# Splitting all weights but four lead-in blocks, and the attention output, in a planned two-layer trunk on one core

## The chip, the cores and the metric

The kernel runs on one core of a Trainium2 chip. The metric is the device time of one execution in microseconds (us), as the median of several runs. A core has five engines that work side by side, each through its own instructions in their written order: TensorE (PE, matrix products; its weight loads are listed as PEld), VectorE (DVE), ScalarE (ACT), GpSimd (POOL) and SyncE (SP, which here issues nearly all DMAs). They meet through semaphores.

## The reference

Two layers of a decoder trunk on 256 tokens of width 1024. Each layer mixes tokens by two attentions side by side (NSA and MoBA, 8 heads of 64 each), merges them by sigmoid gates, and then runs a SwiGLU block of inner width 2816:

```python
for l in range(DEPTH):                                        # 2
    ada = jax.nn.silu(c) @ w_ada[l] + b_ada[l]
    sh_m, sc_m, g_m, sh_f, sc_f, g_f = jnp.split(ada[:, None, :], 6, axis=-1)
    h = rms_norm(x, norm_mix[l]) * (1.0 + sc_m) + sh_m
    (...) = jnp.split(h @ w_in[l], split_at, axis=-1)         # 4888 columns
    y_a = nsa_mixer(...)                                      # 256 x 512
    y_b = moba_mixer(...)                                     # 256 x 512
    gate_a, gate_b = jnp.split(jax.nn.sigmoid(g_br), 2, axis=-1)
    merged = gate_a * (y_a @ w_up_nsa[l]) + gate_b * (y_b @ w_up_moba[l])
    x = x + g_m * (merged @ w_out[l])
    h = rms_norm(x, norm_ffn[l]) * (1.0 + sc_f) + sh_f
    gt, up = jnp.split(h @ w_ffn_in[l], 2, axis=-1)
    x = x + g_f * ((jax.nn.silu(gt) * up) @ w_ffn_out[l])
```

All of it is in 32-bit floats.

## The kernel before

**Units and the two kinds of product.** Tokens lie in two tiles of 128 (t = 0, 1). Weights come from memory in units of 1 MB (128 partitions x 2048), for example four k-blocks of 128 rows by 512 columns, and each k-block times one token tile is one product of 128 x 128 by 128 x 512, added up in a PSUM bank. `load_unit` brings a unit into a tile `raw`. There are two ways on from there:

- A *split* unit goes through `split_unit`: ACT writes `hi`, the weights rounded to the reduced float type fp32r (L631), and DVE writes `lo` = raw - hi (L583). The other operand is kept as such a pair too (`hp` for the normalised input, `mT` for the merged attention, `aT` for the SwiGLU output). `mm3` then makes three fp32r matmuls for one product: hi x hi, hi x lo and lo x hi (L662).
- A *whole* unit is used as it was loaded, in one full fp32 matmul (also L662, in the groups as `raw`), with an operand that is whole too: `hd` for the input, `yy` for the attention output.

Whole are: blocks 0, 2, 4 and 6 of the eight blocks of the lead-in (`WHOLE`), three units of layer 0's input projection (`WHOLE_UNITS`: the second k-half of the columns from 2328, 2840 and 3352), and all eight units of the up-projections (w_up_nsa and w_up_moba, two column halves, two layers). The attention output is copied from PSUM to `yy` by ACT or DVE, whichever the plan gives it to (`evac`, L640 and L641).

**Tiles.** The large tiles (8 KB per partition) are 17 places of an arena, shared by kinds: raw, hi and lo have three places each that any unit may use, and two spare ones for hi and lo (one for raw) that only loads marked `spare` may use, those of w_out and the first of w_ffn_in among them. `yy` takes the first free of places 11 to 14. `aw` holds pieces of w_ada, whose dot products with silu(c) (`ada_dot`, DVE L589) are spread over the program.

**Stages.** In the lead-in, x is normalised (DVE and ACT; the power -0.5 on POOL, L970), silu(c) is spread over all partitions as `crow`, and the eight blocks of w_in's first 1816 columns are multiplied while their share of w_ada is dotted. Then the compression MLP (reads `e`), the rest of w_in (queries, keys, values, gates), both attentions, the up-projections (stage `ups`), w_out, and the FFN; layer 1 goes the same way. While a softmax goes through DVE, ACT and POOL, PE works on weight units of other columns.

**What sets the order.** Operations are recorded first. A planner (`Program.order`) then simulates the engines with a duration for every operation, picks at each step by priority, chooses between the engines that an operation allows, fills PE's planned gaps with matmuls on zeros (`fill`, L456), replays its plan with drawn DMA delays, raises priorities where PE had to wait, and does so 60 times. The best plan is written out engine by engine. So every duration in the planner moves instructions everywhere.

Of the kernel before, what the change touches and what calls it, by code (L numbers as in the profile page):

```python
# [17 lines left out]
P = 128  # L18
# [100 lines left out]
class Op:  # L119
    def __init__(self, no, alts, key):  # L120
        self.no, self.alts, self.key = no, alts, key
        self.preds, self.succs, self.acc, self.new = {}, [], [], []
        self.bytes = 0
        self.level = 0.0
        self.stage, self.first, self.boost = None, False, 0.0
        self.func, self.loads, self.parts, self.paced, self.then = None, None, False, False, None
# [5 lines left out]
FIRST = 1000.0  # L132
LAT = {"PE": 0.24, "DVE": 0.09, "ACT": 0.09, "POOL": 0.2, "SP": 0.0, "Q": 0.0}
# [5 lines left out]
class Program:  # L139
# [9 lines left out]
    SWITCH = (0.0, 0.0, 0.1)  # L149
# [116 lines left out]
    def order(self):  # L266
# [24 lines left out]
        parts = False  # L291
# [43 lines left out]
        while left:  # L335
# [6 lines left out]
            for op in ready:  # L342
# [15 lines left out]
            for e, cs in per.items():  # L358
# [44 lines left out]
            if e == "PE":  # L403
                parts = op.parts
# [14 lines left out]
            else:  # L419
                free[e] = t + c  # L420
# [21 lines left out]

    def fill(self, t0, t1):
# [15 lines left out]
        op.stage = "fill"  # L459
# [20 lines left out]
    def replay(self, steps, seed):  # L480
# [4 lines left out]
        dma, table, parts, gaps = 0.0, (), False, []  # L485
        for i, (e, op, c, deps) in enumerate(steps):
# [5 lines left out]
            if e == "PE":  # L492
                if op.stage != "fill" and op.parts != parts:
                    parts = op.parts
                    idle += self.SWITCH[2]
# [13 lines left out]
            free[e] = t + c  # L509
# [49 lines left out]
class Engines:  # L559
# [25 lines left out]
    def stt(self, out, a, s, b, op0, op1, accum=None):  # L585
# [5 lines left out]
                  [a, s, b], [out] + list(kw.values()), extra=0.08 if kw else 0.0)  # L591

    def ttr(self, out, a, b, op0, op1, init, accum):
        self._vec(("DVE",), cols(out), True,
                  lambda v: v.tensor_tensor_reduce(AP(out), AP(a), AP(b), 1.0, init, op0, op1, AP(accum)),  # L595
                  [a, b], [out, accum], extra=0.08)

    def ts(self, out, a, s1, s2, op0, op1=None, engs=("DVE",)):
# [3 lines left out]
                  [a, s1, s2], [out], psum=self._psum(a))  # L602
# [12 lines left out]
    def act(self, out, a, func, scale=None, bias=None, accum=None, late=()):  # L615
# [27 lines left out]
    def mm(self, out, lhsT, rhs, start, stop, cost=None):  # L643
# [6 lines left out]
        op.parts = AP(lhsT).shape[0] < P or AP(out).shape[0] < P  # L650

    def term(self, out, lhsT, rhs, first):
# [13 lines left out]
        self.p.op({"PE": (cost, [go])}, [lhsT, rhs], [out], term=s)  # L666

    def tr(self, out, a, ident):
        self.p.op({"PE": (0.109, [lambda: self.nc.tensor.transpose(AP(out), AP(a), AP(ident))])}, [a, ident], [out])  # L669

    def dma(self, out, src, q="SP", least=60000):
# [5 lines left out]
        eng = {"SP": self.nc.sync, "POOL": self.nc.gpsimd}[q]  # L677
        return self.p.op({q: (0.43 if q == "SP" else 0.6, [lambda: eng.dma_start(AP(out), AP(src))])},  # L678
# [5 lines left out]
WHOLE_UNITS = {(0, c, 1) for c in (2328, 2840, 3352)}  # L684


HALVED = 1
# [15 lines left out]
def trunk_kernel(tc, pools, A):  # L703
# [33 lines left out]
    NB = 17  # L737
# [16 lines left out]
    arena("yy", (11, 12, 13, 14), inturn=True)  # L754
# [373 lines left out]
    def lead_in(bs, h, W):  # L1128
# [16 lines left out]
        dma(vecs, A["vecs"], q="POOL")  # L1145
# [68 lines left out]
    def sublayer_mix(l, h):  # L1214
# [4 lines left out]
        ev, kv_, qv, vv, yv = (R.val(x_) for x_ in ("e", "kk", "qq", "ve", "yy"))  # L1219
# [185 lines left out]
        def softmax_T(s, t, nh, rq_small, cols_, gate):  # L1405
# [21 lines left out]
            alts["ACT"] = (nh * (0.295 + nk / 1200),  # L1427
# [47 lines left out]
        def nsa(t):  # L1475
# [43 lines left out]
            yaT[t] = whole_piece(quarter(yv, t, t), y)  # L1519

        def moba(t):
# [31 lines left out]
            ybT[t] = whole_piece(quarter(yv, 2 + t, 2 + t), y)  # L1553
# [72 lines left out]
        log_soon([yv, *tgv.values()])  # L1626
# [8 lines left out]
    def resid(l, t, c, b, g, e0=0, e1=512):  # L1635
# [3 lines left out]
        with R.ahead():  # L1639
            tt(r, b.of(e0)[:, e0:e1] if e1 - e0 < 512 else b, g[:, cs_], ALU.mult)  # L1640
# [6 lines left out]
    def sublayer_ffn(l, h):  # L1647
# [153 lines left out]
```

## Time and profile before

| | |
|---|---|
| median of 3 runs | 816.95 us (816.85 to 820.06) |
| span of the profiled execution | 815.4 us |
| granted TensorE clock | 1.000 |
| PE, busy share of the span | 99% |
| weight loads (PEld) | 75% |
| DVE | 71% |
| ACT | 50% |
| POOL | 10% |
| DMA moved | 183.82 MB, 225 GB/s on average |

The profiled execution's own time is known as its span, from the first to the last instruction; the median of the runs is 1.55 us above it. In the rows of the trace, a group names line, engine, operation and tiles (out<-in, without their numbers), then how many, their busy time, the mean of one, and the engine's idle time before them with what ended it. A timeline row gives start and length in us. Matmuls are pipelined: their lengths overlap, so the time of one is read from the distance between starts. A full fp32 matmul has two records.

### The profile page before, as it was taken

The numbers are of one execution on the slowest core, as the hardware profiler recorded it, in microseconds if no ns is written. First come the engines' busy times: TensorE is split into PE (matmuls) and PEld (weight loads), VectorE is DVE, ScalarE is ACT, GpSimd is POOL, SyncE is SP. The second block draws the span as 40 slices with busy tenths as digits, with TensorE's granted clock in tenths as the row PEclk, the third lists the DMA queues.
The fourth block names the chain that finished last, engine by engine and source line by source line (L and its number), as shares of the span: only waits on it lengthen the run. The fifth ranks groups of instructions, "written<-read, shape, count | busy, mean of one in ns | idle before, by whom it ended". The sixth has DMA issues, their size and how long they took to land.

```text
span 815.4 us, 10543 instructions
## 1 busy us (share of the span) xinstructions
PE 803.8 (99%) x3997; PEld 610.0 (75%) x3997; DVE 580.2 (71%) x1025; ACT 410.3 (50%) x654; POOL 79.5 (10%) x75
## 2 busy tenths in 40 slices
PE   8999999999999999999999999999999999999997
PEld 4567656764878888888878887676477888889886
DVE  6889977677986877777788898776377526545454
ACT  5445366662673534433585566587347524433441
POOL 4702620000100000000000442000000000000000
PEclk9999999999999999999999999999999999999999
DMA  9967585538949887977855785540391645555441
GB/s 357 416 230 290 161 295 182 175 130 310 372 152 338 311 305 288 327 293 259 311 174 214 278 289 180 188 151 25 104 344 69 210 153 174 202 192 207 151 158 52
DMA packets 74018, 183.82 MB, mean 225 GB/s; under 512 B 4304, under 2 KB 9696, under 8 KB 73456
## 3 DMA queue, kind: packets, MB, share of 16 engines
q1 hardware_dynamic: 73920, 183.08, 63.0%
q8 instruction: 31, 0.51, 0.2%
q14 instruction: 19, 0.16, 0.1%
q0 software_dynamic: 48, 0.08, 0.0%
HBM read 182.10 MB, written 1.05 MB: 225 GB/s over the span
## 4 chain that ended last, share of the span: by engine, by line
PE 88%; DVE 4%; DMA 2%; ACT 2%; POOL 2%; issue 1%; SPq 0%; DVEq 0%; POOLq 0%
PE bank L662 77%; PE bank L648 6%; PE bank L669 5%; DMA rows<-in_rows 1%; DVE tmp L583 1%; DMA raw<-in_w_out 1%; DVE lo L583 1%; POOL tmp L601 1%; DVE tmp L601 1%; ACT hp L631 1%; ACT hi L631 1%; SPq L678 0%; POOL tmp L583 0%; POOL at L1431 0%; DVE e L583 0%
## 5 line engine op out<-in xcount | busy, mean ns | idle before, releaser
L662 PE MATMUL bank<-hi,hp 128*128 128x512 f32 (+2 forms) x1296 | 359.2, 384 | 2.2 <-DVE hp L583 1.5
L583 DVE TENSOR_TENSOR lo<-raw,hi 128x2048 fp32r<-128x2048 f32 (+2 forms) x107 | 240.4, 2261 | 104.7 <-ACT hi L631 103.8
L631 ACT ACTIVATE hi<-raw 128x2048 fp32r<-128x2048 f32 (+2 forms) x107 | 200.6, 1891 | 223.1 <-PE bank L662 181.9
L662 PEld LDWEIGHTS bank<-hi,hp 128*128 128x128 f32 x1296 | 234.1, 188 | 59.1 <-issue 7.0
L662 PE MATMUL bank<-lo,hp 128*128 128x512 f32 (+2 forms) x648 | 208.2, 383 | 0.3 <-DVE lo L583 0.2
L662 PEld LDWEIGHTS bank<-lo,hp 128*128 128x128 f32 x648 | 119.3, 188 | 24.1 <-issue 2.6
L589 DVE SCALAR_TENSOR_TENSOR aw<-aw,crow 128x1024 f32<-128x1024 f32 x80 | 96.2, 1220 | 7.5 <-DMA aw<-in_w_ada 7.3
L662 PE MATMUL bank<-hi,aT 128*128 128x512 f32 (+1 forms) x364 | 100.7, 387 | 0.0
L662 PEld LDWEIGHTS bank<-hi,aT 128*128 128x128 f32 x364 | 66.6, 188 | 13.5 <-ACT hi L631 1.0
L662 PE MATMUL bank<-raw,yy 128*128 128x512 f32 x128 | 58.7, 596 | 0.7 <-ACT yy L640 0.7
L662 PE MATMUL bank<-lo,aT 128*128 128x512 f32 (+1 forms) x182 | 58.0, 385 | 0.0
L662 PE MATMUL bank<-raw,hd 128*128 128x512 f32 (+1 forms) x112 | 49.6, 568 | 0.9 <-ACT hd L631 0.9
L662 PEld LDWEIGHTS bank<-raw,yy 128*128 128x128 f32 x128 | 23.0, 190 | 23.7 <-issue 21.8
L662 PE MATMUL bank<-hi,mT 128*128 128x512 f32 x128 | 39.9, 403 | 0.1
L662 PEld LDWEIGHTS bank<-lo,aT 128*128 128x128 f32 x182 | 34.1, 188 | 6.1
L669 PE MATMUL bank<-ident,tmp 128*128 128x128 f32 x256 | 37.5, 274 | 1.2 <-DVE tmp L985 0.7
L631 ACT ACTIVATE at<-at,nb,rqa 128x128 f32<-128x128 f32 (+1 forms) x64 | 34.2, 536 | 7.5 <-DVE nb L589 7.5
L669 PEld LDWEIGHTS bank<-ident,tmp 128*128 128x128 f32 x256 | 30.4, 140 | 9.8 <-issue 1.8
L595 DVE CUSTOM_DVE_ANT_0 at<-bank,maskf 128x128 f32<-128x128 f32 (+1 forms) x96 | 29.5, 352 | 11.3 <-PE bank L669 8.9
L662 PEld LDWEIGHTS bank<-raw,hd 128*128 128x128 f32 x112 | 20.6, 189 | 17.2 <-issue 13.4
L583 DVE TENSOR_TENSOR tmp<-tmp,bank 128x512 f32<-128x512 f32 (+1 forms) x24 | 15.1, 639 | 22.0 <-PE bank L662 21.5
L631 ACT ACTIVATE tmp<-bank 128x512 f32<-128x512 f32 (+2 forms) x43 | 20.7, 509 | 16.3 <-PE bank L662 7.0
(185 smaller groups left out, 731.3 us busy)
## 6 DMA issues: line engine op xcount, KB each, us to landing
raw<-in_w_ffn_in SPq DMA_DIRECT2D x44, 1024.0 KB, 6.3
aw<-in_w_ada SPq DMA_DIRECT2D x80, 512.0 KB, 5.7
raw<-in_w_in SPq DMA_DIRECT2D x30, 1024.0 KB, 5.2
raw<-in_w_ffn_out SPq DMA_DIRECT2D x22, 1024.0 KB, 4.9
raw<-in_w_out SPq DMA_DIRECT2D x8, 1024.0 KB, 6.2
raw<-in_w_in SPq DMA_DIRECT2D x8, 908.0 KB, 9.1
sa<-in_w_ada SPq DMA_DIRECT2D x7, 1024.0 KB, 11.9
raw<-in_w_up_nsa SPq DMA_DIRECT2D x4, 1024.0 KB, 6.2
```

Of the source, the lines that this page charges most:

```text
L583: self._vec(engs, cols(out), True, lambda v: v.tensor_tensor(AP(out), AP(a), AP(b), op=op), [a, b], [out])
L589: lambda v: v.scalar_tensor_tensor(AP(out), AP(a), AP(s), AP(b), op0=op0, op1=op1, **{k: AP(x) for k, x in kw.items()}),
L595: lambda v: v.tensor_tensor_reduce(AP(out), AP(a), AP(b), 1.0, init, op0, op1, AP(accum)),
L601: lambda v: v.tensor_scalar(AP(out), AP(a), AP(s1), AP(s2), op0=op0, **kw),
L631: op = self.p.op({"ACT": (c, [lambda: self.nc.scalar.activation(AP(out), AP(a), func, **{k: AP(x) for k, x in kw.items()})])}, reads + lis ...
L648: op = self.p.op({"PE": (cost, [lambda: self.nc.tensor.matmul(AP(out), AP(lhsT), AP(rhs), start=start, stop=stop)])}, [lhsT, rhs], [out])
L662: self.nc.tensor.matmul(AP(out), AP(lhsT), AP(rhs), start=first, stop=v.gone == v.terms)
L669: self.p.op({"PE": (0.109, [lambda: self.nc.tensor.transpose(AP(out), AP(a), AP(ident))])}, [a, ident], [out])
```

## The change

It does six things. `WHOLE_UNITS` becomes empty and the up-projections' units are loaded split (`UPS_WHOLE`). The attention output is written as a pair by `split_into` (ACT writes hi, DVE lo), in two tiles `yy`, for which the arena gets an 18th place. The constants `vecs` are loaded through ACT's queue instead of POOL's. The planner gets other durations: a cost for each change of the matmul's shape in partitions, 0.08 and 0.1 us by which DVE and ACT take the next operation before the last one's result is there, and other costs of single operations. The last quarter of the result, which was multiplied in two halves of 256 columns, is multiplied in one piece of 512 again, and only its final scaling and adding stay halved. And the memory set aside for descriptors of software DMAs is cut to 2048 bytes.

```diff
+OVER = {"PE": 0.0, "DVE": 0.08, "ACT": 0.1, "POOL": 0.0, "SP": 0.0, "Q": 0.0}
...
-    SWITCH = (0.0, 0.0, 0.1)
+    TURN, SLACK, TALL = 0.15, 0.0, 0.05
+    FLAT, STICK = (P, P), 0.0
...
+            if e == "PE" and op.forms:
+                if op.forms[0] != form:
+                    t = max(t, free[e] + self.turn(form, op.forms[0]))
+                form = op.forms[1]
...
-                free[e] = t + c
+                free[e] = t + c - OVER[e]
...
-        eng = {"SP": self.nc.sync, "POOL": self.nc.gpsimd}[q]
-        return self.p.op({q: (0.43 if q == "SP" else 0.6, [lambda: eng.dma_start(AP(out), AP(src))])},
+        eng = {"SP": self.nc.sync, "ACT": self.nc.scalar}[q]
+        return self.p.op({q: (0.43 if q == "SP" else 0.15, [lambda: eng.dma_start(AP(out), AP(src))])},
...
-WHOLE_UNITS = {(0, c, 1) for c in (2328, 2840, 3352)}
+WHOLE_UNITS = set()
+UPS_WHOLE = (False, False)
...
-    NB = 17
+    NB = 18
...
-    arena("yy", (11, 12, 13, 14), inturn=True)
+    arena("yy", (17, 11, 12, 13, 14), inturn=True)
...
-        dma(vecs, A["vecs"], q="POOL")
+        dma(vecs, A["vecs"], q="ACT")
...
-        def whole_piece(d, src):
-            evac(d, src)
-            return [(None, None, d[:, j * P:(j + 1) * P]) for j in range(4)]
+        yl = None if UPS_WHOLE[l] else R.val("yy", dt=F32R)
+
+        def y_pieces(i, src):
+            d = quarter(yv, i, i)
+            if yl is None:
+                evac(d, src)
+                return [(None, None, d[:, j * P:(j + 1) * P]) for j in range(4)]
+            return split_into(d, quarter(yl, i, i), src)
...
-            yaT[t] = whole_piece(quarter(yv, t, t), y)
+            yaT[t] = y_pieces(t, y)
...
-                u = load_unit(A[w][l][:, cs_], 4, 512, True)
+                u = load_unit(A[w][l][:, cs_], 4, 512, UPS_WHOLE[l])
...
-            keys += [(i, t, k, c, e) for t in range(NT) for c in range(2) for e in parts[(t, c)]
-                     for i in range(nu - nl, nu) for k in range(2)]
+            keys += [(i, t, k, c) for t in range(NT) for c in range(2) for i in range(nu - nl, nu) for k in range(2)]
...
-    nc = bacc.Bacc("TRN2", target_bir_lowering=False, num_devices=1)
+    nc = bacc.Bacc("TRN2", target_bir_lowering=False, num_devices=1, dynamic_dma_scratch_size=2048)
```

Three places show how instructions move. A trailing number tells tiles of one kind apart.

The first is PE at the end of layer 0's attention: the last two of the products with the attention weights (`pt`) and the values (`ve`), and the up-projections behind them. Before:

```order
L648 MATMUL bank_68<-pt_85,ve_772 64x128
L648 MATMUL bank_68<-pt_84,ve_772 64x128
L662 MATMUL bank_65<-raw_1155,yy_1177 128x512
L662 MATMUL bank_64<-raw_1211,yy_1177 128x512
L662 MATMUL bank_65<-raw_1211,yy_1177 128x512 x4
L662 MATMUL bank_64<-raw_1321,yy_1177 128x512
L662 MATMUL bank_63<-raw_1321,yy_1177 128x512 x4
```

Now (yy_1188 is the output's hi part, yy_1198 its lo part):

```order
L659 MATMUL bank_68<-pt_85,ve_774 64x128
L659 MATMUL bank_68<-pt_84,ve_774 64x128
L678 MATMUL bank_64<-hi_1527,yy_1198 128x512
L678 MATMUL bank_64<-hi_1527,yy_1188 128x512
L678 MATMUL bank_64<-lo_1545,yy_1188 128x512
L678 MATMUL bank_64<-hi_1527,yy_1198 128x512
L678 MATMUL bank_65<-lo_1545,yy_1188 128x512
```

Each whole matmul has become three that need hi and lo of the weights and of the output, and they may stand apart from each other.

The second is DVE at the same place: the dot products (`aw`), the gated merge (`tmp<-tg,bank`), and the splits. Before:

```order
L589 SCALAR_TENSOR_TENSOR aw_73,mod_f_138<-aw_73,crow_101 128x1024
L589 SCALAR_TENSOR_TENSOR aw_72,mod_f_138<-aw_72,crow_101 128x1024
L589 SCALAR_TENSOR_TENSOR aw_74,mod_f_138<-aw_74,crow_101 128x1024
L589 SCALAR_TENSOR_TENSOR tmp_75<-tg_1194,bank_64 128x512
L583 TENSOR_TENSOR lo_1597<-raw_1567,hi_1584 128x2048
L589 SCALAR_TENSOR_TENSOR mT_1595<-bank_70,mT_1595 128x512
```

Now:

```order
L593 TENSOR_TENSOR lo_1545<-raw_1140,hi_1527 128x2048
L624 RECIPROCAL ri_197<-rs_190 128x2
L1450 TENSOR_TENSOR at_82<-at_82,ri_197 128x512
L593 TENSOR_TENSOR lo_1571<-raw_1290,hi_1556 128x2048
L624 RECIPROCAL ri_196<-rs_191 128x2
L599 SCALAR_TENSOR_TENSOR aw_72,mod_f_138<-aw_72,crow_101 128x1024
L599 SCALAR_TENSOR_TENSOR aw_73,mod_f_138<-aw_73,crow_101 128x1024
L599 SCALAR_TENSOR_TENSOR aw_74,mod_f_138<-aw_74,crow_101 128x1024
L593 TENSOR_TENSOR lo_1627<-raw_1374,hi_1612 128x2048
L593 TENSOR_TENSOR yy_1198<-bank_68,yy_1188 128x512
```

Three of the four up-projection units of the layer (lo_1545, lo_1571, lo_1627) are split between the last softmax's steps and ahead of the output's own lo part.

The third is the start, on POOL and DVE: `posf` is the cast of the positions, which come with `vecs`; `rx` are the norms' powers; `sa` are dot products. POOL before:

```order
L808 MEMSET vbd_116 128x128
L808 MEMSET vbd_115 128x128
L970 TENSOR_TENSOR rx_132<-rx_132,mhalf_100 128x1
L605 CAST posf_136<-vecs_104 128x3
L970 TENSOR_TENSOR rx_133<-rx_133,mhalf_100 128x1
```

POOL now:

```order
L826 MEMSET vbd_116 128x128
L826 MEMSET vbd_115 128x128
L616 CAST posf_136<-vecs_104 128x3
L988 TENSOR_TENSOR rx_132<-rx_132,mhalf_100 128x1
L988 TENSOR_TENSOR rx_133<-rx_133,mhalf_100 128x1
```

DVE before:

```order
L985 TENSOR_SCALAR tmp_76<-x_102,rx_132 128x512
L601 TENSOR_SCALAR rx_133<-ssx_125,ssx_129 128x1
L589 SCALAR_TENSOR_TENSOR sa_214,mod_m_137<-sa_214,crow_101 128x1024
L985 TENSOR_SCALAR tmp_78<-x_103,rx_133 128x512
L589 SCALAR_TENSOR_TENSOR sa_214,mod_m_137<-sa_214,crow_101 128x1024
```

DVE now:

```order
L611 TENSOR_SCALAR ssx_129<-ssx_125 128x1
L611 TENSOR_SCALAR rx_133<-ssx_125,ssx_129 128x1
L1003 TENSOR_SCALAR tmp_76<-x_102,rx_132 128x512
L599 SCALAR_TENSOR_TENSOR sa_217,mod_m_137<-sa_217,crow_101 128x1024 x2
L593 TENSOR_TENSOR mod_m_137<-mod_m_137,vecs_104 128x2
```

The cast moved ahead of the first power, and on DVE the scaling of x (L1003) stands between the second power's input and the first dot product; before, the dot product followed that input at once.

More of the change, by code (lines that the diff above doesn't have):

```diff
@@ L125, in __init__ @@
         self.stage, self.first, self.boost = None, False, 0.0
-        self.func, self.loads, self.parts, self.paced, self.then = None, None, False, False, None
+        self.func, self.loads, self.forms, self.paced, self.then = None, None, None, False, None
     def rank(self, e):
@@ L290, in order @@
         table = ()
-        parts = False
+        form = self.FLAT
         parked, aside = {}, set()
@@ L441, in order, with turn @@
         return out
+    def turn(self, a, b):
+        return self.TURN + (self.TALL if b[0] < P <= b[1] else 0.0)
     def fill(self, t0, t1):
@@ L484, in replay @@
         start, end, by = [], [], []
-        dma, table, parts, gaps = 0.0, (), False, []
+        dma, table, form, gaps = 0.0, (), self.FLAT, []
         for i, (e, op, c, deps) in enumerate(steps):
@@ L492, in replay @@
             if e == "PE":
-                if op.stage != "fill" and op.parts != parts:
-                    parts = op.parts
-                    idle += self.SWITCH[2]
+                if op.forms and op.forms[0] != form:
+                    idle += self.turn(form, op.forms[0])
+                if op.forms:
+                    form = op.forms[1]
                 if idle < self.COLD and op.stage != "fill":
@@ L508, in replay @@
             by.append(who)
-            free[e] = t + c
+            free[e] = t + c - OVER[e]
             if e == "SP":
@@ L601, in ts @@
                   lambda v: v.tensor_scalar(AP(out), AP(a), AP(s1), AP(s2), op0=op0, **kw),
-                  [a, s1, s2], [out], psum=self._psum(a))
+                  [a, s1, s2], [out], psum=self._psum(a),
+                  extra=0.12 if self._psum(a) and isinstance(s1, Ref) else 0.0)
     def copy(self, out, a, engs=("DVE",)):
@@ L649, in mm, with formed @@
                                                                     stop=stop)])}, [lhsT, rhs], [out])
-        op.parts = AP(lhsT).shape[0] < P or AP(out).shape[0] < P
+        self.formed(op, AP(lhsT).shape[0], AP(out).shape[0])
+    @staticmethod
+    def formed(op, k, m):
+        f = tuple(next(w for w in (32, 64, P) if n <= w) for n in (k, m))
+        op.forms = (op.forms[0] if op.forms else f, f)
     def term(self, out, lhsT, rhs, first):
@@ L1218, in sublayer_mix @@
         qbT, vb, rqb = {}, {}, {}
-        ev, kv_, qv, vv, yv = (R.val(x_) for x_ in ("e", "kk", "qq", "ve", "yy"))
+        ev, kv_, qv, vv = (R.val(x_) for x_ in ("e", "kk", "qq", "ve"))
+        yv = R.val("yy", dt=None if UPS_WHOLE[l] else F32R)
         E = [quarter(ev, i, i) for i in range(2)]
@@ L1639, in resid @@
         with R.ahead():
-            tt(r, b.of(e0)[:, e0:e1] if e1 - e0 < 512 else b, g[:, cs_], ALU.mult)
+            tt(r, b[:, e0:e1], g[:, cs_], ALU.mult)
             xx = x[t].of(c)
```

48 lines of the change are left out of this document (22 added, 26 removed).

## The prediction

> **What bounds the kernel now.** I read the page's busy times first, then the chain that ended last, then the groups by shape, then the timeline of TensorE (PE) where the two kinds of product run.
>
> ```profile
> span 815.4 us, 10543 instructions
> ...
> PE 803.8 (99%) x3997; PEld 610.0 (75%) x3997; DVE 580.2 (71%) x1025; ACT 410.3 (50%) x654; POOL 79.5 (10%) x75
> ...
> PE bank L662 77%; PE bank L648 6%; PE bank L669 5%; DMA rows<-in_rows 1%; DVE tmp L583 1%; DMA raw<-in_w_out 1%; DVE lo L583 1%; POOL tmp L601 1%; DVE tmp L601 1%; ACT hp L631 1%; ACT hi L631 1%; SPq L678 0%; POOL tmp L583 0%; POOL at L1431 0%; DVE e L583 0%
> ```
>
> PE is busy 803.8 of 815.4 us, and the weight products (L662) alone make 77% of the chain that ended last. No wait is worth much. What counts is how long PE takes for its work, and whether a change leaves it without work. Two kinds of weight product run on it, whole and split:
>
> ```profile
> L662 PE MATMUL bank<-raw,yy 128*128 128x512 f32 x128 | 58.7, 596 | 0.7 <-ACT yy L640 0.7
> ...
> L662 PE MATMUL bank<-raw,hd 128*128 128x512 f32 x96 | 46.8, 596 | 0.9 <-ACT hd L631 0.9
> ```
>
> ```profile
> 593.50 3.59 PE L662 MATMUL bank<-raw,yy 128*128 128x512 f32 x8
> 596.93 0.27 PE L669 MATMUL bank<-ident,tmp 128*128 128x128 f32 x1
> ```
>
> ```profile
> 182.59 13.39 PE L662 MATMUL bank<-raw,yy 128*128 128x512 f32 x30
> 195.83 0.60 PE L669 MATMUL bank<-ident,tmp 128*128 128x128 f32 x4
> ```
>
> ```profile
> 631.94 73.62 PE bank L662 x324
> ```
>
> The means (596 ns) overlap one another, since matmuls are pipelined, so I take the distance between starts. A whole product is written as one matmul and appears as two records: the 64 up-projection products give the 128 records of the first row. Eight records took 596.93 - 593.50 = 3.43 us, 0.429 each; thirty took 13.24, 0.441 each. One whole product is 0.858 to 0.882 us. The chain's row of 324 split matmuls in the second layer's FFN gives 73.62 / 324 = 0.2272 each, and a split product has three: 0.682.
>
> **Products.** The change turns 88 whole products 512 wide into split ones: 64 up-projections (2 layers x 2 column halves x 2 weights x 4 k-blocks x 2 token tiles), and 24 of layer 0's input projection (3 units of 4 x 2), which are half of the 96 records with hd; the lead-in's own stay. So 88 x (0.858 - 0.682) = 15.5 us less, up to 88 x (0.882 - 0.682) = 17.6. I take 15.5: the eight records are an undisturbed run, the thirty span other instructions' ends.
>
> Does a third weight load eat this?
>
> ```profile
> L662 PEld LDWEIGHTS bank<-raw,yy 128*128 128x128 f32 x128 | 23.0, 190 | 23.7 <-issue 21.8
> ...
> L662 PEld LDWEIGHTS bank<-hi,mT 128*128 128x128 f32 x128 | 23.5, 188 | 5.2 <-issue 0.5 <-ACT hi L631 0.3
> ```
>
> A load takes the same 0.19 us for either kind and is shorter than the 0.2272 between split matmuls, so 88 more loads hide under the matmuls, as they do in the 324. [...]
>
> **The tail.** The last bank's matmuls were 256 wide and become 512 wide again.
>
> ```profile
> 810.24 0.40 PE L662 MATMUL bank<-hi,aT 128*128 128x256 f32 x2
> ...
> 810.60 0.28 PE L662 MATMUL bank<-hi,aT 128*128 128x256 f32 x1
> 810.92 0.76 DVE L583 TENSOR_TENSOR tmp<-bank,gbc 128x256 f32<-128x256 f32 x2 [0.43 <-PE bank L662]
> 811.59 0.75 DVE L583 TENSOR_TENSOR x<-x,tmp 128x256 f32<-128x256 f32 x2
> ```
>
> Three narrow ones (two in the first row, one between) take 810.60 - 810.24 = 0.36, so 36 take 4.3 us, against 18 x 0.2272 = 4.1: 0.2 less. Behind the last matmul the same two multiplies and two adds run as before, and the same output DMA. Nothing else moves there: 0.
>
> **The start.** The constants' DMA leaves POOL's queue for ACT's, and the cast of the positions, which waits for it, now stands ahead of both powers that the norms need.
>
> ```profile
> vecs<-in_vecs POOLq DMA_DIRECT2D x1, 81.5 KB, 5.4
> ```
>
> ```profile
> 1.43 0.77 POOL L678 DMA_DIRECT2D vecs<-in_vecs  x1
> ...
> 2.57 0.21 ACT L631 ACTIVATE ccol<-ccol 128x8 f32<-128x8 f32 x1 [0.57 <-DMA ccol<-in_c]
> ...
> 6.48 0.58 POOL L970 TENSOR_TENSOR rx<-rx,mhalf 128x1 f32<-128x1 f32 x1 [2.52 <-DVE rx L601]
> ...
> 8.11 1.23 DVE L589 SCALAR_TENSOR_TENSOR sa<-sa,crow 128x1024 f32<-128x1024 f32 x1
> 8.22 1.53 POOL L970 TENSOR_TENSOR rx<-rx,mhalf 128x1 f32<-128x1 f32 x1 [0.91 <-DVE rx L601]
> ...
> 12.64 0.70 PE L662 MATMUL bank<-raw,hd 128*128 128x512 f32 x1 [0.45 <-ACT hd L631]
> ```
>
> On ACT the issue delays the table load by at most POOL's 0.77; ACT's first activation waits 0.57 for its input anyway, so up to 0.2 shows. If the landing still takes 5.4 us from an issue at about 0.7 to 1.5 us, the cast is ready at 6.1 to 6.9 and the first power, at 6.48, can be 0.4 + 0.3 late. Against that, the second power took 1.53 us and the first 0.58. It started inside a dot product on DVE (8.11 to 9.34) and ended 0.4 after it. In the new order a short DVE instruction stands between, so 0.95 can go. I take 0, with ends of -0.95 and +0.9. [...]
>
> **What the splits cost.** Every split weight unit is one copy on ACT and one subtraction on DVE.
>
> ```profile
> L583 DVE TENSOR_TENSOR lo<-raw,hi 128x2048 fp32r<-128x2048 f32 x101 | 229.6, 2288 | 101.5 <-ACT hi L631 100.6 <-PE bank L662 0.4
> L631 ACT ACTIVATE hi<-raw 128x2048 fp32r<-128x2048 f32 x101 | 191.5, 1913 | 219.8 <-PE bank L662 181.9 <-DMA raw<-in_w_out 29.2 <-issue 5.2
> ...
> L589 DVE SCALAR_TENSOR_TENSOR aw<-aw,crow 128x1024 f32<-128x1024 f32 x80 | 96.2, 1220 | 7.5 <-DMA aw<-in_w_ada 7.3
> ...
> L583 DVE TENSOR_TENSOR aT<-bank,aT 128x512 fp32r<-128x512 f32 x20 | 13.2, 684 | 4.2 <-ACT aT L631 4.2
> ...
> L1426 DVE TENSOR_TENSOR at<-at,ri 128x512 f32<-128x512 f32 x21 | 14.5, 692 | 0.7
> ...
> L641 DVE COPY pt<-bank 128x512 f32<-128x512 f32 x10 | 6.9, 690 | 9.7 <-PE bank L669 8.2 <-ACT yy L640 1.5
> ```
>
> ```profile
> 58.50:215.50 157.00, 155.91 (x813) 102.13 (x812) 127.60 (x312) 86.11 (x185) 29.74 (x21) 1.00 0.67 235
> 436.90:604.70 167.80, 166.72 (x919) 120.60 (x918) 125.86 (x311) 95.52 (x196) 23.47 (x12) 1.00 0.53 183
> ```
>
> ```profile
> PE bank L662 <- DVE lo L583: 0.2, 1, 0.2
> ...
> ACT hi L631 <- PE bank L662: 181.9, 44, 10.8
> ```
>
> The two window rows (columns: length, then busy time of PE, weight loads, DVE, ACT, POOL) are the attention stretches, from the first write of e to the last write of mT on DVE. In layer 0 DVE is busy 127.6 of 157.0 us, in layer 1 125.9 of 167.8. Counted in the two orders between these writes, layer 0 has 8 more subtractions (18.3 us), 3 fewer dot products (-3.7), 4 subtractions of the attention output in place of 2 copies (2.7 - 1.4), 3 more copies (2.1), 3 fewer normalisations (-2.1) and 2 fewer adds of about 0.69 (-1.4): 14.5 more, 142.1 in all. PE's share of the stretch shrinks by 56 products x 0.176 = 9.9, to 147.1. DVE would be 97% busy. Layer 1 gets 7 subtractions, 1 dot product, 4 subtractions of outputs, 2 copies, less 3 normalisations: 19.3, so 145.2 of 167.8 - 5.6 = 162.2, 90%. ACT gets 8 x 1.91 = 15.3 in layer 0 and stays far below the stretch.
>
> What hides this is the store of split units. The hi copies waited 181.9 us for a slot that PE still used: up to three units (the slots that these loads may use) lay ready, each good for 8 x 0.682 = 5.5 us of PE, and PE waited 0.2 us in all for a lo. This cover thins in layer 0, where 4.9 us of DVE's time stay free instead of 29.4. From below the cost is 0 (PE is fed as now); from above it is what the first rival makes of it. I take 2 us, nearer to the row of PE's waits on lo than to the other end, because DVE's idle time today is mostly its wait for PE, which shrinks when splits queue up. [...]
>
> The later parts of an attention output split (0.68 us on DVE behind the ACT copy) have cover in layer 1: ten split matmuls, 2.3 us, now stand between the last attention product and the first up-projection, where one of 0.7 us was waited for. 0. The 18th arena tile takes the output's hi part, its lo part goes where the whole output lay: no slot is lost, 0.
>
> **Sum.** 815.4 - 15.5 - 0.2 + 2.0 = 801.7 us of span. The median shown is 816.95, 1.55 above the profiled span, so I forecast 803.2. About 0.5%, 4.1 us, is what a measurement can tell: faster means under 812.9, slower over 821.0.
>
> **Rivals.** First, slower: DVE becomes the bound of layer 0's attention. It needs 142.1 us there; if it must stay idle as long as today (29.4, waits for PE's scores and transposes inside the softmax chains), the stretch takes 171.5 instead of 147.1, 24.4 more, and the time is 816.95 - 15.7 + 24.4 = 825.7. It decides from an idle time of 4.9 + 15.7 = 20.6 us on. For it: 97%. Against it: the waits in which DVE idles now are waits in which the new splits can run, and ACT took over three normalisations. 0.04.
>
> Second, no change that can be told: the eight up-projection units each make PE wait for one lo (2.29), 18.3 us, and the time is 819.6. For it: the whole weights were PE's filler while the softmax ran, needing neither DVE nor ACT, and the new fillers need both. Against it: in the new order three up units' subtractions stand ahead of the output's, so they are early. With three or four units late it is 808 to 810. All eight, or most: 0.05; five or so, 810 to 812.9: 0.05.
>
> Third, a larger gain: whole products at 0.882 (17.6), the second power shorter (0.95), no new wait: 816.95 - 17.8 - 0.95 = 798.2. Below 798, where the truer durations also close gaps of the old plan: 0.07.
>
> **Chances.** My forecast, 798 to 810: 0.79, and that is the range; 0.07 lie below and 0.14 above. Faster 0.79 + 0.07 + 0.05 = 0.91, same 0.05, slower 0.04.
>
> **What would show it.** Right: no records of raw with yy, 64 products more with hi and lo of yy at 0.227 between starts; PE's share still about 99%; DVE near 140 us in layer 0's stretch, which is some 8 us shorter; the two FFNs as long as now; the last 4.5 us unchanged. Wrong: waits of PE for lo or for softmax results adding up to 10 us or more between the lead-in and the first layer's output projection, a first weight product later than 13.5 us, or split matmuls with yy further apart than 0.24.

## The result, and the profile after

The changed kernel takes 805.81 us (median of 4 runs, 805.06 to 809.33) beside 818.5 us before (4 runs, 816.85 to 824.0): a ratio of 0.9855 (the median over all pairs of a run before and a run after) with a 95% interval of 0.9824 to 0.9886. It is faster, by 12.7 us. The profiled executions differ by 815.4 - 803.3 = 12.1.

The head of the page of the changed kernel:

```profile
span 803.3 us, 10733 instructions
...
PE 787.8 (98%) x4062; PEld 623.5 (78%) x4062; DVE 601.1 (75%) x1034; ACT 436.0 (54%) x688; POOL 75.3 (9%) x73
```

PE is still the bound, but its share fell from 99% to 98%: its work shrank more than the span did. The new products, by shape and in a piece of PE's timeline:

```profile
L678 PE MATMUL bank<-hi,yy 128*128 128x512 f32 x128 | 40.2, 396 | 0.0
L678 PE MATMUL bank<-lo,yy 128*128 128x512 f32 x64 | 23.7, 390 | 0.0
```

```profile
175.04 0.40 PE L678 MATMUL bank<-lo,yy 128*128 128x512 f32 x1
175.28 0.40 PE L678 MATMUL bank<-hi,yy 128*128 128x512 f32 x1
175.51 0.39 PE L678 MATMUL bank<-lo,yy 128*128 128x512 f32 x1
```

No record of raw with yy is left. The split ones start 0.23 apart. Now the two attention stretches, from the first write of e to the last of mT on DVE (length, then busy time of PE, weight loads, DVE, ACT, POOL):

```profile
59.83:207.47 147.64, 142.60 (x849) 109.11 (x848) 140.28 (x311) 101.23 (x204) 28.17 (x19) 1.00 0.72 250
425.68:594.23 168.55, 167.89 (x974) 130.52 (x973) 142.42 (x322) 108.55 (x211) 21.44 (x12) 1.00 0.58 201
```

Layer 0's stretch is 9.4 us shorter than before, with DVE busy for 95% of it. What PE waited for between 45 and 115 us, around the end of the lead-in and the compression MLP, first before the change:

```profile
PE bank L648 <- DVE e L583: 0.4, 1, 0.4
PE bank L669 <- POOL at L1431: 0.3, 1, 0.3
```

And after it:

```profile
PE bank L685 <- DVE kbd_tok L611: 1.4, 1, 1.4
PE bank L659 <- DVE e L593: 1.3, 1, 1.3
PE bank L685 <- DVE e L593: 0.7, 1, 0.7
PE bank L685 <- ACT e L651: 0.6, 1, 0.6
PE bank L685 <- DVE rqa L611: 0.5, 1, 0.5
PE bank L685 <- DVE tmp L593: 0.3, 1, 0.3
PE bank L678 <- DVE lo L593: 0.3, 1, 0.3
```

That is 5.1 us instead of 0.7. Over the whole span PE's waits add up to 10.7 us, 6.6 before. So about 4 us of the gain were given back, and at this place. Only 0.3 of it is a wait for a lo.

One more row matters for what follows. The last products of the attention weights and the values (`pt`, `ve`) show when PE gets the end of the last softmax. Layer 0 before and after (the last two times are the starts of the first and the last):

```profile
L648 PE MATMUL bank<-pt,ve x48: 272/273/323, 170.6 to 182.4; 128*64 128x128 f32 x48
```

```profile
L659 PE MATMUL bank<-pt,ve x48: 272/273/323, 159.2 to 174.3; 128*64 128x128 f32 x48
```

They end 8 us earlier, although DVE has more to do.

### The profile page after: what moved, and what is told of

Its sections match the earlier page's. It is cut to its first block, busy times and chain, and to the rows that moved or that the text cites. A ratio compares the mean times of both kernels' runs of the same rounds, so it can differ in the third digit from the quotient of the medians.

```text
span 803.3 us, 10733 instructions
## 1 busy us (share of the span) xinstructions
PE 787.8 (98%) x4062; PEld 623.5 (78%) x4062; DVE 601.1 (75%) x1034; ACT 436.0 (54%) x688; POOL 75.3 (9%) x73
## 4 chain that ended last, share of the span: by engine, by line
PE 67%; DVE 5%; ACT 1%; issue 1%; DVEq 0%; ACTq 0%
PE bank L678 61%; PE bank L685 4%; PE bank L659 2%; DVE lo L593 2%; DVE tmp L593 1%; ACT at L642 1%; DVE ss L620 0%; DVE x L593 0%; DVE aw L599 0%; ACT hi L642 0%; DVE at L605 0%; DVE e L593 0%; ACT hp L642 0%; DVE mT L599 0%; DVE tmp L599 0%
## 5 line engine op out<-in xcount | busy, mean ns | idle before, releaser
L678 PE MATMUL bank<-hi,hp 128*128 128x512 f32 (+2 forms) x1344 | 375.6, 383 | 1.6 <-ACT hp L642 0.9
L593 DVE TENSOR_TENSOR lo<-raw,hi 128x2048 fp32r<-128x2048 f32 (+2 forms) x118 | 268.8, 2295 | 121.7 <-ACT hi L642 120.2
L642 ACT ACTIVATE hi<-raw 128x2048 fp32r<-128x2048 f32 (+2 forms) x118 | 221.3, 1893 | 211.8 <-PE bank L678 189.8
L678 PE MATMUL bank<-lo,hp 128*128 128x512 f32 (+2 forms) x672 | 219.8, 382 | 0.3 <-DVE lo L593 0.3
L678 PE MATMUL bank<-hi,aT 128*128 128x512 f32 x352 | 100.4, 394 | 0.3 <-ACT aT L642 0.3
L678 PE MATMUL bank<-lo,aT 128*128 128x512 f32 x176 | 56.7, 392 | 0.0
L678 PE MATMUL bank<-hi,yy 128*128 128x512 f32 x128 | 40.2, 396 | 0.0
L593 POOL TENSOR_TENSOR tmp<-tmp,tmp 128x512 f32<-128x512 f32 (+2 forms) x12 | 13.7, 1139 | 176.4 <-DVE tmp L599 158.1
L678 PEld LDWEIGHTS bank<-hi,yy 128*128 128x128 f32 x128 | 24.0, 188 | 6.0 <-issue 0.5
L678 PEld LDWEIGHTS bank<-hi,mT 128*128 128x128 f32 x128 | 23.8, 188 | 6.1 <-DVE mT L599 1.6
```

Of the source, the lines that this page charges most:

```text
L593: self._vec(engs, cols(out), True, lambda v: v.tensor_tensor(AP(out), AP(a), AP(b), op=op), [a, b], [out])
L642: op = self.p.op({"ACT": (c, [lambda: self.nc.scalar.activation(AP(out), AP(a), func, **{k: AP(x) for k, x in kw.items()})])}, reads + lis ...
L678: self.nc.tensor.matmul(AP(out), AP(lhsT), AP(rhs), start=first, stop=v.gone == v.terms)
```

## The experiments

Twelve kernels ran. In the table "zeros" is the number of matmuls on zeros (`zb` with `zb`, which the plan puts into gaps that it foresees for PE), "last pt" the start of layer 0's last pt-ve product, and "waits" PE's waits between 45 and 115 us and in the whole span. Each ratio is to runs of the kernel before taken beside that kernel, whose medians were 818.0 to 818.5 us.

| kernel | us (median) | ratio to before, 95% | zeros | last pt | waits |
|---|---|---|---|---|---|
| before | 818.5 | | 27 | 182.4 | 0.7 / 6.6 |
| changed | 805.81 | 0.9855 (0.9824 to 0.9886) | 22 | 174.3 | 5.1 / 10.7 |
| 1 splits, old durations | 825.46 | 1.0084 (1.0072 to 1.0097) | 63 | 190.1 | 2.0 / 15.8 |
| 2 new durations alone | 824.83 | 1.0082 (1.0068 to 1.0095) | 24 | 175.4 | 5.7 / 11.7 |
| 3 up-projections whole | 821.17 | 1.0039 (1.0025 to 1.0054) | 23 | 173.9 | 6.9 / 14.5 |
| 4 input units whole | 812.57 | 0.9930 (0.9918 to 0.9942) | 24 | 177.1 | 5.9 / 13.4 |
| 5 no overlap | 818.29 | 1.0002 (0.9992 to 1.0012) | 36 | 186.2 | 2.4 / 17.8 |
| 6 splits and overlap only | 815.99 | 0.9974 (0.9963 to 0.9984) | 43 | 185.1 | 3.7 / 11.0 |
| 7 other draws | 809.40 | 0.9892 (0.9880 to 0.9905) | 22 | 176.5 | 5.8 / 14.7 |
| 8 e first | 810.82 | 0.9911 (0.9897 to 0.9926) | 25 | 178.8 | 5.7 / 13.5 |
| 9 late overlap | 803.76 | 0.9822 (0.9806 to 0.9839) | 27 | 173.3 | 2.9 / 8.0 |
| 10 rc first | 810.46 | 0.9902 (0.9885 to 0.9919) | 22 | 177.2 | 4.1 / 12.7 |
| 11 overlap of DVE only | 814.09 | 0.9945 (0.9925 to 0.9964) | 25 | 190.2 | 8.7 / 15.5 |
| 12 late overlap, other draws | 806.09 | 0.9851 (0.9835 to 0.9868) | 28 | 176.3 | 1.0 / 8.7 |

The first theory (A) was the prediction's: PE's work falls by 15.7 us whatever the plan, and the plan only decides which few us of waits come back. The rivals were that DVE's further subtractions cost PE (B), and that the planner's durations bring the gain (C).

**1. The splits with the old durations**, that is, from the kernel before:

```diff
-WHOLE_UNITS = {(0, c, 1) for c in (2328, 2840, 3352)}
+WHOLE_UNITS = set()
+UPS_WHOLE = (False, False)
...
-    NB = 17
+    NB = 18
...
-        dma(vecs, A["vecs"], q="POOL")
+        dma(vecs, A["vecs"], q="ACT")
```

with the split attention output and the last quarter in one piece, and every duration as before.

> The kernel before with all the edits of data and tiles (split weights, split attention output, 18th place, constants on ScalarE's queue, the last quarter in one piece), planned with the old durations. Theory A (PE's work fell by 15.7 us, and 3.6 us came back as waits of PE between 55 and 95 us because the new plan ends layer 0's lead-in in another order): the work falls by the same 15.7 us, and what comes back is the old plan's own: 0.981 to 0.985 of the time before, so 803 to 806 beside 818.5. Rival B (DVE's 15 further subtractions make PE wait, whatever the plan): 0.985 or above, with PE waiting 3 us or more for DVE in layer 0. Rival C (the planner's truer durations bring most of the gain): above 0.99, over 810 us.

It is slower than before: 825.46 us, 1.0084. Theory A fell here: PE has 15.7 us less work by the forecast's prices, and the kernel takes 7 us more. B's window and C's both hold it. Layer 0's last softmax in this kernel, on PE's timeline:

```profile
183.48 1.90 PE L456 MATMUL bank<-zb 128*128 128x512 bf16 x8
186.04 0.63 PE L669 MATMUL bank<-ident,at 128*128 128x128 f32 x4 [0.66 <-DVE at L1433]
186.50 1.03 PE L456 MATMUL bank<-zb 128*128 128x512 bf16 x4
...
189.28 1.09 PE L648 MATMUL bank<-pt,ve 128*64 128x128 f32 x14 [0.33 <-ACT pt L640]
191.37 0.66 PE L669 MATMUL bank<-ident,tmp 128*128 128x128 f32 x4 [1.01 <-DVE tmp L583]
```

PE multiplies zeros and waits for single steps of the softmax (`at`, `pt`): it has run out of weight products before the softmax is done, which ends at 190.1 instead of 182.4. The group of the zeros has 63 matmuls here and 22 in the changed kernel:

```profile
L456 PE MATMUL bank<-zb 128*128 128x512 bf16 x63 | 17.0, 412 | 1.0 <-DVE zb L809 1.0
```

```profile
L465 PE MATMUL bank<-zb 128*128 128x512 bf16 x22 | 6.1, 436 | 1.0 <-DVE zb L826 1.0
```

Eight zeros took 1.90 us, the last one's tail included, so one is about 0.22. 41 more are 9 us, and PE's waits are 5.1 longer than in the changed kernel: 14 of the 19.6 us between the two. The rest shows in the distances between starts: the weight products take no longer here than in the changed kernel (688.3 against 691.0 us), all that is longer lies at the zeros (14.5 us) and at the transposes and the other small products (7.4), the waits behind them included. The zeros stand in the order, so the planner foresaw these gaps; 30 of them lie in layer 0's stretch and 11 in layer 1's.

**2. The new durations alone**, from the kernel before (with the last quarter in one piece):

```diff
+OVER = {"PE": 0.0, "DVE": 0.08, "ACT": 0.1, "POOL": 0.0, "SP": 0.0, "Q": 0.0}
...
-                free[e] = t + c
+                free[e] = t + c - OVER[e]
...
-    SWITCH = (0.0, 0.0, 0.1)
+    TURN, SLACK, TALL = 0.15, 0.0, 0.05
```

> The kernel before with the planner's new durations alone (and the last quarter in one piece, 0.2 us of PE's work). Theory A: PE's work is as before, so 0.998 to 1.005 of the time before; if the new durations themselves cause the waits at the end of the lead-in, they show here too, with 2 to 5 us of PE's waits between 50 and 110 us against 0.4 us before. Rival B (splits on DVE cause the waits): within 0.3% of before and no more than 1 us of waits between 50 and 110 us. Rival C: below 0.994, a gain of 5 us or more.

Slower too, 824.83 us, above A's window as well. The waits between 45 and 115 us are there (5.7), as in the changed kernel, so they belong to the new durations and not to the splits: that part of A holds, and B is out as their cause. They are most of what this kernel loses: over the whole span PE waits 5.1 us longer than before the change. C as put is out as well, since the durations bring nothing by themselves. But they do move something. DVE's and ACT's busy time from 160 to 200 us, before:

```profile
160.00:180.00 20.00, 20.00 (x126) 12.88 (x125) 14.62 (x45) 14.11 (x43) 0.00 (x0) 1.00 0.29 85
180.00:200.00 20.00, 19.99 (x66) 9.30 (x65) 12.82 (x19) 4.87 (x5) 0.00 (x0) 1.00 0.88 320
```

and in this kernel:

```profile
160.00:180.00 20.00, 20.00 (x131) 15.83 (x130) 11.24 (x27) 13.90 (x34) 0.00 (x0) 1.00 0.49 184
180.00:200.00 20.00, 20.00 (x48) 8.70 (x47) 7.44 (x14) 1.88 (x2) 0.00 (x0) 1.00 0.45 170
```

DVE has 18.7 us of work left there instead of 27.4: the softmaxes are through 7 us earlier (175.4 against 182.4). With whole up-projections that is worth nothing here: in this stretch PE has no listed wait in either kernel. So two edits that each cost about 7 us gain 12.7 together.

**3. and 4. Parts of the change undone.** The up-projections whole again, and layer 0's three units whole again:

```diff
-UPS_WHOLE = (False, False)
+UPS_WHOLE = (True, True)
```

> The changed kernel with the up-projections and the attention output whole again (64 products more at 0.858 instead of 0.682 us). Theory A: PE's work grows by 11.3 us and the waits at the lead-in's end stay: 805.8 + 11.3 = 817.1, 0.998 of the time before (0.995 to 1.001). Rival B (DVE's load costs PE): 8 subtractions of 2.29 us and 8 of 0.68 us leave DVE, PE's waits fall by 3 us or more: 814 or less, below 0.995.

```diff
-WHOLE_UNITS = set()
+WHOLE_UNITS = {(0, c, 1) for c in (2328, 2840, 3352)}
```

> The changed kernel with layer 0's three input-projection units whole again (24 products, 24 x 0.176 = 4.2 us more work of PE, 3 subtractions less on DVE). Theory A (order of the plan): 805.8 + 4.2 = 810.0, 0.990 of the time before, give or take 1.5 us for the order of another plan. Rival D (those three units needed no split and so covered the stretch behind the lead-in; without them PE ran dry there): the waits between 50 and 110 us fall from 5.1 to about 1 us and the time stays at 805 to 807, 0.985.

821.17 and 812.57 us, 15.4 and 6.8 more than the changed kernel. 64 and 24 products at 0.176 are 11.3 and 4.2; PE's waits grew by 3.8 and 2.7. The sums, 15.1 and 6.9, meet the measured ones. So the price of a product was right. Both missed A's windows by those waits. B, as the cause of the changed kernel's waits, and D are refuted: with fewer splits PE waits more, not less.

**5. The changed kernel without the overlap.** The theory now (F): the planner's old durations take each DVE instruction for 0.08 us longer than it needs (two subtractions of 2.28 us took 4.48, last section). With the further splits its plan holds DVE for the bound, lets the softmaxes end late, and leaves PE without work. The rival (G): plans differ by chance.

```diff
-OVER = {"PE": 0.0, "DVE": 0.08, "ACT": 0.1, "POOL": 0.0, "SP": 0.0, "Q": 0.0}
+OVER = {"PE": 0.0, "DVE": 0.0, "ACT": 0.0, "POOL": 0.0, "SP": 0.0, "Q": 0.0}
```

> The changed kernel with the planner's overlap set to zero (the 0.08 us of DVE and 0.10 us of ACT by which the next operation may start before the last one's end); all other new durations stay. Work of PE as in the changed kernel, but the plan now holds 36 matmuls on zeros instead of 22 and ends layer 0's softmaxes later. Theory F (the overlap is what makes the split kernel's plan work: about 310 DVE instructions of an attention x 0.08 = 25 us that the planner otherwise takes for busy): the last product of pt and ve in layer 0 starts at 180 us or later instead of 174.3, PE loses 5 to 15 us around the end of the attentions, 811 to 821 us, 0.991 to 1.003 of the time before. Rival G (no term of the durations matters by itself, plans differ by chance): 803 to 809.

818.29 us: the whole gain is gone, by two numbers of the planner. Layer 0's softmax ends as late as F said:

```profile
L658 PE MATMUL bank<-pt,ve x48: 272/273/324, 171.8 to 186.2; 128*64 128x128 f32 x48
```

and PE waits for it, the longest waits from 150 to 215 us:

```profile
PE bank L684 <- DVE at L1449: 1.6, 2, 1.1
PE bank L684 <- DVE tmp L592: 1.6, 1, 1.6
PE bank L658 <- ACT pt L650: 1.4, 3, 0.9
```

In the changed kernel PE has no listed wait between 150 and 200 us.

**6. The splits with the overlap alone**, that is the first kernel with `OVER` and the two lines that use it:

> The kernel of the first run (all edits of data and tiles, old durations) with the overlap of DVE and ACT alone added to the planner. The plan holds 43 matmuls on zeros instead of 63. Theory F: most of the 20 us between that run (825.5) and the changed kernel (805.8) comes back: 809 to 815, 0.988 to 0.996 of the time before, with excess left where the zeros stand in layer 1's attention. Rival G: 820 to 828, about where the first run was. Rival H (ACT's lower price for a normalisation, which moves softmax steps from DVE to ACT, is what brings it): above 818.

815.99 us, a little above F's window: 9.5 of the 19.6 us come back, by the overlap alone. G and H are out. Of its 43 zeros 15 stand in layer 1's attention, as F said, and its last pt comes only 5 us earlier than in run 1. The rest belongs to the other durations (the price of a change of shape, of ACT's normalisation, of accumulators); which of them was not tried.

**7. Other draws of the DMA delays** for the planner's replay:

```diff
-            runs = [self.replay(steps, seed) for seed in range(self.RUNS)]
+            runs = [self.replay(steps, seed) for seed in range(100, 100 + self.RUNS)]
```

> The changed kernel, planned with another eight draws of the DMA delays: same durations, another order everywhere. Theory F: the result belongs to the durations, 803 to 810 us, 0.981 to 0.990 of the time before, with the same 22 matmuls on zeros and the last product of pt and ve in layer 0 at 172 to 178 us. Rival G (chance of the plan): it may be off by 8 us or more, 814 and above.

809.40 us, same zeros, last pt at 176.5. F's window holds, and it gives the size of chance: 3.6 us between two plans of one kind.

**8. and 10. Priority for two paths at the end of the lead-in.** In run 8 `R.boost = 40.0` stands around the copy, transposes and writes that make `e` in layer 0; in run 10 around the power `rc` and the writes of `kbd_tok`.

> The changed kernel with a higher priority (40) for layer 0's path into the compression MLP: the copy of keys and values on ACT, its transposes and the eight writes of e on DVE. Theory A2 (the 5 us of PE's waits between 50 and 110 us come from that path standing behind other small DVE steps): waits there fall from 5.1 to 3 us or less, 802.5 to 804.5 us, 0.980 to 0.983. Rival A3 (they come from when the lead-in's last banks are finished and from how much other work PE has left then): waits stay at 4 to 6 us and the time at 805 to 808.

> The changed kernel with a higher priority (40) in layer 0 for the compressed keys' norm: its power rc on POOL and the writes of kbd_tok behind it. In the changed kernel that power stood behind another, rkb, that took 3.61 us under two subtractions of DVE, and PE waited 1.4 us for kbd_tok. Theory A6 (that queue on POOL is a cause by itself): the wait for kbd_tok goes, 804 to 805 us, 0.981 to 0.983. Rival A5 (chance from plan to plan): 805 to 811 with other waits in its place.

810.82 and 810.46 us. In run 8 `e` still cost 2.1 us and `kbd_tok` 2.3. In run 10 the wait for `kbd_tok` went from 1.4 to 0.3, but those for `tmp` grew from 0.3 to 1.2, and a softmax step on POOL cost 2.5 us between 150 and 200 us. A2 and A6 gained nothing: the wait for `kbd_tok` fell only in run 10, and others grew. But the waits are the smaller part of the loss. In both profiled executions the TensorE clock was at 0.50 for 6.8 us (last section), which costs PE an estimated 3.4; together with 2.8 and 2.0 us more of waits and 0.7 and 0 of zeros that is 6.9 and 5.4 of the 7.5 and 5.5 us by which their spans exceed the changed kernel's. With runs 7, 8 and 10, the changed kernel's 805.81 is the best of four plans of its kind. Run 7's profile has no such stretch, so its 3.6 us are those of the order.

**9. and 12. Overlap only from the attention on.** Layer 0's writes of `e` do not overlap (0.438 us between starts, 0.418 long; last section), so the planner's 0.08 is too much there. The edit leaves it out for every operation of the stages up to the compression MLP.

```diff
+EARLY = ("lead", "0grpA", "0postA", "0post", "0mlp")
...
-                free[e] = t + c - OVER[e]
+                free[e] = t + c - (0.0 if op.stage in EARLY else OVER[e])
```

> The changed kernel with the overlap left out of the plan for the operations of the lead-in, of layer 0's steps behind it and of its compression MLP; from layer 0's attention on it stays. The plan then holds 27 matmuls on zeros (5 more, 1.1 us, between 40 and 70 us). Theory A4 (the waits between 50 and 110 us come from the overlap being put on for operations that do not show it, the writes of e above all: they start 0.43 us apart and last 0.42): PE's waits there fall from 5.1 to 2 to 3 us as in the run without overlap, the attention stays as in the changed kernel, 802 to 805 us, 0.978 to 0.983 of the time before. Rival A5 (these waits differ from plan to plan by chance, as between the runs so far): 805 to 811, no better than the changed kernel.

803.76 us, the fastest here, with 2.9 us of waits between 45 and 115 us, inside A4's window. Since four plans of one kind had differed by 5 us, the same was planned with the draws of run 7:

> The kernel of the ninth run (overlap from layer 0's attention on only), planned with another eight draws of the DMA delays, as the seventh run was to the changed kernel (809.4). Theory A4 (leaving the overlap out at the lead-in removes waits there whatever the plan): waits of PE between 45 and 115 us at 2 to 3.5 us, and 803 to 807 us, 0.981 to 0.987 of the time before, so at least 2.4 us below the seventh run. Rival A5 (the ninth run was a lucky plan among plans that differ by 5 us): 807.5 to 812.

806.09 us, 3.3 below run 7, whose interval (0.9880 to 0.9905) does not touch this one's (0.9835 to 0.9868). The waits between 45 and 115 us, 1.0 in all, less than A4 said:

```profile
PE bank L686 <- ACT e L652: 0.5, 1, 0.5
PE bank L679 <- DVE lo L594: 0.3, 1, 0.3
PE bank L686 <- DVE tmp L594: 0.2, 1, 0.2
```

That leaving the overlap out there gains holds in both pairs (2.0 and 3.3 us); the intervals of run 9 and the changed kernel overlap, so that pair alone would not show it. That it is the writes of `e` that matter, as A4 has it, is not shown: no run left the overlap out for them alone.

**11. Overlap for DVE alone.**

```diff
-OVER = {"PE": 0.0, "DVE": 0.08, "ACT": 0.1, "POOL": 0.0, "SP": 0.0, "Q": 0.0}
+OVER = {"PE": 0.0, "DVE": 0.08, "ACT": 0.0, "POOL": 0.0, "SP": 0.0, "Q": 0.0}
```

> The changed kernel with the overlap for DVE alone (0.08), none for ACT. Theory F1 (DVE's load is what the planner took for too high; ACT has room): most of the 12.5 us between the changed kernel and the run without any overlap comes back, 806 to 810 us, 0.983 to 0.989 of the time before. Theory F2 (the two stand in one chain, softmax steps on ACT between steps on DVE, so that each shortens it): about half comes back, 810 to 815, 0.989 to 0.996, and the last product of pt and ve in layer 0 starts between 176 and 184 us.

814.09 us, in F2's window, but not by F2's picture. The last pt product starts at 190.2, later than forecast, and there PE waits only 0.3 us between 150 and 200 us; the loss stands between 45 and 115 us: 8.7 us of waits, 3.6 more than in the changed kernel (`kbd_tok` 3.0 and a step on POOL 2.8 the largest), and behind these two waits the TensorE clock at 0.50 for 3.4 and 6.8 us (last section), an estimated 5.1 more. That is 8.7 of the 10.5 us by which this profiled span, 813.8, is longer. So a late end of the softmax costs only where PE lacks weight products at that time. How much each of the two numbers brings is left open, the more so as this kernel's runs went from 811.04 us at a mean clock of 0.998 to 816.68 at 0.992.

## Why the prediction was right, and where it was not

**Products: right.** 88 products at 0.176 less. Runs 3 and 4 give the same price from the other side.

**Tail: right.** Between the last matmul's start and the end lie 803.3 - 798.51 = 4.8 us, as before (815.4 - 810.60), with the same two multiplies and adds:

```profile
798.51 0.39 PE L678 MATMUL bank<-hi,aT 128*128 128x512 f32 x1
798.95 0.75 DVE L593 TENSOR_TENSOR tmp<-bank,gbc 128x256 f32<-128x256 f32 x2
799.62 0.75 DVE L593 TENSOR_TENSOR x<-x,tmp 128x256 f32<-128x256 f32 x2
```

**Start: at the lower end.** I took 0 out of -0.95 to +0.9. The constants and the powers of the norm, in the changed kernel:

```profile
vecs<-in_vecs ACTq DMA_DIRECT2D x1, 81.5 KB, 2.2
```

```profile
2.96 0.40 POOL L616 CAST posf<-vecs 128x3 f32<-128x3 int32 x1
6.41 0.58 POOL L988 TENSOR_TENSOR rx<-rx,mhalf 128x1 f32<-128x1 f32 x1 [3.05 <-DVE vecs L611]
7.99 0.74 POOL L988 TENSOR_TENSOR rx<-rx,mhalf 128x1 f32<-128x1 f32 x1 [0.99 <-DVE rx L611]
```

```profile
11.74 3.31 PE L678 MATMUL bank<-raw,hd 128*128 128x512 f32 x8 [0.35 <-ACT hd L642]
```

The DMA landed 2.2 us after its issue instead of 5.4, so the cast was long done. The second power took 0.74 instead of 1.53, and the first weight product came at 11.74 instead of 12.64. By the first write of `e` nothing of this 0.9 is left (59.83 against 58.51). The queue was not tried alone.

**What the splits cost: size nearly right, place and reason wrong.** DVE's load came out as worked out, 140.3 of 147.6 us in layer 0 (142.1 of 147.1 forecast) and 142.4 in layer 1 (145.2). I put +2.0 for PE's waits on `lo`; it was about 4, and not for `lo`. They come from the new durations (run 2), at the end of the lead-in, and fall when the overlap is left out there (runs 5, 9 and 12). The prediction gave the durations no term. The length of layer 0's stretch, 147.6 us beside 147.1, is closer than it should be: it holds 849 matmuls where 813 before, 56 more and the 4 zeros less make 865, so 16 of them, an estimated 3.6 us, stand elsewhere.

**"What hides this is the store of split units": the step that failed.** The units were ready, and PE hardly waited for them (0.3 us), but in run 1 they were nearly as ready (1.3 us of waits on hi and lo) and the kernel was slower than before. What hid the splits was that the softmaxes ended early enough for PE still to have weight products beside them, and that came from the planner's new durations: without the overlap the whole gain is gone (run 5), and alone it brings about half (run 6). The sum was read from an order in which this was already settled, so it could come right without this step. How near it came is in part luck: another plan with the same durations (run 7) gave 809.40, at the edge of the range of 798 to 810.

**Layer 1 and the FFNs.** Layer 1's stretch was to be 5.6 us shorter and is 0.8 longer (168.55 against 167.80). The parts that were to stay are shorter instead: between the stretches 218.2 instead of 221.4, behind the second 209.1 instead of 210.7. Work moved across the bounds: layer 1's stretch holds 974 matmuls, where 919 and 32 more make 951, and 23 at 0.2272 are an estimated 5.2 of the 6.4 us that it is off.

**The rivals.** The first, DVE as the bound (825.7), did not happen in the changed kernel, where DVE was busy for 95% of layer 0's stretch. Run 1 shows its picture at its time (825.46), with a 163.0 us stretch where 171.5 was worked out, and there the order made it, not DVE's speed: with the changed kernel's durations the same splits go through. The second did not happen: 0.3 us of waits on `lo`. Of the third, only the shorter second power came.

**POOL beside the subtractions.** Behind the start the forecast has no term for POOL. One of POOL's powers of eight columns and what stood behind it:

```profile
84.78 3.61 POOL L966 TENSOR_TENSOR rkb<-rkb,mhalf 128x8 f32<-128x8 f32 x1 [0.70 <-DVE rkb L611]
88.36 1.81 POOL L1412 TENSOR_TENSOR rc<-rc,mhalf 64x1 f32<-64x1 f32 x1
```

```profile
84.62 2.28 DVE L593 TENSOR_TENSOR lo<-raw,hi 128x2048 fp32r<-128x2048 f32 x1
...
87.48 2.27 DVE L593 TENSOR_TENSOR lo<-raw,hi 128x2048 fp32r<-128x2048 f32 x1
90.20 0.71 DVE L611 TENSOR_SCALAR kbd_tok<-tmp,rc 32x64 f32<-32x64 f32 x1 [0.44 <-POOL rc L1412]
```

The power took 3.61 us beside two subtractions, where the shortest of its width takes 1.63; `rc` waited in POOL's order behind it and took 1.81 beside the second subtraction, `kbd_tok` waited for `rc`, and PE 1.4 us for `kbd_tok`. The power ends 1.49 us, and `rc` 0.42, behind the subtraction inside which it began. Of the changed kernel's twelve powers of this width ten began inside a DVE instruction that reads no bank; they ended 1.49 to 1.50 us behind its end and took 1.89 to 3.63. The other two, one begun inside no DVE instruction and one inside one that reads a bank (`tmp<-bank,ct`), took 1.63. A subtraction held up by a power is not seen here: the second one began 0.9 us before the power's recorded end and took 2.27.

## What to carry to other kernels

Where a planner orders the work, an edit of the work and an edit of its durations are one change: time each alone and both together before crediting either. Price an instruction of a chain by the distance to the next start, not by its recorded length (two subtractions of 2.28 us took 4.48 here), and check the planner's number against that. When PE's work shrinks, look first at when the longest chain beside it ends, and at the matmuls on zeros: they count the gaps that the plan itself foresaw. And behind a long wait of PE (2.3 to 3.0 us here) read the granted clock (0.50 for 3.4 or 6.8 us here) before putting the whole loss down to the wait.

## What the runs showed of the hardware

In this trace instructions on DVE and on ACT start before the one ahead has ended. Two subtractions on DVE, each 2.28 long, and two copies on ACT, 1.90 and 1.92:

```profile
105.15 4.48 DVE L593 TENSOR_TENSOR lo<-raw,hi 128x2048 fp32r<-128x2048 f32 x2
```

```profile
103.08 3.72 ACT L642 ACTIVATE hi<-raw 128x2048 fp32r<-128x2048 f32 x2 [1.50 <-PE bank L678]
```

2 x 2.28 - 4.48 is 0.08, and 1.90 + 1.92 - 3.72 is 0.10. This is the overlap that the planner's two numbers stand for.

Layer 0's writes of `e` are an exception:

```profile
61.04 2.61 DVE L593 TENSOR_TENSOR e<-bank,vecs 64x256 f32<-64x256 f32 x6
...
63.58 0.67 DVE L593 TENSOR_TENSOR tmp<-bank,ct 128x512 f32<-128x512 f32 x1
```

```profile
L593 DVE TENSOR_TENSOR e<-bank,vecs x16: 406/418/430, 59.8 to 448.0; 64x256 f32<-64x256 f32 x16
```

The six start (2.61 - 0.418) / 5 = 0.438 apart and last 0.418; the instruction behind them starts 0.07 before the last one's end. They go by turns to partitions 0 to 63 and 64 to 127. In layer 1 the second and third write both go to 64 to 127, and there the third starts at 426.45, 0.08 before the second (426.10, 0.43 long) ends; the first and the fourth go to 0 to 63 and start 0.42 before the second and 0.43 behind the third, without overlap. That the partitions are what holds them apart was not tried by itself.

Behind some waits of PE the granted clock was 0.50. In run 11 (columns as in the stretches above; the last three are the granted clock and two of the DMA):

```profile
105.58 0.27 PE L685 MATMUL bank<-ident,kbd_tok 64*128 64x64 f32 x1 [3.01 <-DVE kbd_tok L611]
...
110.80 2.33 PE L678 MATMUL bank<-hi,hp 128*128 128x512 f32 x5
112.94 0.90 PE L678 MATMUL bank<-lo,hp 128*128 128x512 f32 x2
```

```profile
106.70:113.50 6.80, 6.80 (x23) 5.42 (x22) 5.65 (x15) 3.38 (x5) 0.00 (x0) 0.50 0.47 157
```

For 6.8 us the clock is 0.50, and split matmuls start (112.94 - 110.80) / 5 = 0.43 us apart instead of 0.23. The same comes behind run 11's wait of 2.78 us and run 10's of 2.55 (3.4 us at 0.50 each) and run 8's of 2.31 (6.8 us). A wait of 2.06 us in run 8 has no such stretch behind it, while in run 10 one follows two waits of 0.71 and 1.26, so the runs do not show what sets it. The changed kernel's profile has none; of its four runs the slowest, 809.33 us, had a mean clock of 0.996, and the others, 805.06 to 806.19, had 0.998 to 1.000.
